# Hybrid decoder block on one core: query, key and all gate projections moved into seven-product units, attention heads moved behind them

## The chip, the cores and the metric

The kernel runs on one core of one Trainium2 chip. The metric is the device time in microseconds (us) of one execution, taken as the median of the runs. A core has five engines with a queue each, and each queue runs in order: TensorE (PE, matrix products and transposes; PEld is its load of the stationary operand), VectorE (DVE), ScalarE (ACT), GpSimd (POOL) and SyncE (SP), which issues every DMA of this kernel. Work on different engines meets only through semaphores.

## The reference, cut to what matters

One block, 1024 tokens, width 1024, float32:

```python
xn = rmsnorm(x, norm1_g)
qa, ka, va, qr, kr, vr, gr, gate_a, gate_b = [xn @ wl[:, bounds[i]:bounds[i + 1]] for i in range(9)]
qa = rmsnorm(qa.reshape(B, S, 12, 128), q_norm_g); ka = rmsnorm(ka.reshape(B, S, 12, 128), k_norm_g)
# three groups of four heads: query t attends keys t - j*dilation, (window, dilation) = (128,1), (512,4), (2048,16)
s = q @ k.T * 128**-0.5 - slope * distance        # -inf outside the window
m = max(s); p = exp(s - m); den = sum(p); o = p @ v / den; lse = m + log(den)
o_a = sum over the groups of softmax(lse over the groups) * o
o_r = groupnorm(retention(qr, kr, vr)) * silu(gr)
y = sigmoid(gate_a) * (o_a @ w_proj_a) + sigmoid(gate_b) * (o_r @ w_proj_b)
x = x + y @ w_out
x = x + square(relu(rmsnorm(x, norm2_g) @ w_up)) @ w_down
```

The combined projection `wl` has 12,800 columns: queries, keys and values of attention 1536 each, retention queries and keys 1024 each, retention values and its gate `gr` 2048 each, `gate_a` and `gate_b` 1024 each.

## The kernel before

**Products.** Each operand of a large product is held as two parts, a rounded one and the rest (`split`, L325 to L330: ACT writes the rounded part `wh` or `xh`, DVE subtracts for `wl` or `xl`), and each 128-deep term is three matmuls (`Pipe.group`, L229): high by high, high by low, low by high. All large matmuls carry line 229. `mm`, `ms` and `tr` are PSUM pools of three, two and three banks (`mm` 3, `tr` 2, `ms` 3).

**Two forms of a projection.** The plain form takes every term. The other is a unit of seven products for 256 output columns over all 1024 tokens: the token and depth halves of the input form sums and differences once (`differences`, operands `ES`), the weight quarters form theirs per unit (`sums`, L123), and the seven products N1 to N7 (`strassen_order`, `product`) are added up into the four quarters of the result. A product is 4 terms, 12 matmuls of 512 columns; a unit is 84 of them, where the plain form of the same columns takes 96. `Weights` loads, sums and splits the weights in the order that is written out for it, through three or four raw slots and six split buffers.

**Order.** PE runs in the order in which the program is written (`manual_schedule`); the other engines are ordered by a scheduler. `Pipe.at(lag, fn)` puts a small piece of work between the terms of a later step, so that PE has large matmuls to run while DVE and ACT prepare it. The stages up to the retention are these:

1. Attention: 12 heads (`heads`: slot by slot, groups 1, 2, 0), 8 blocks of 128 tokens each. A step computes queries, keys and values of one head and one block in plain form (24 matmuls, 384 columns). ACT sums the squares of queries and keys (L659), DVE and POOL make the root (L342, L343), DVE scales (L663), PE turns them (L669), ACT and DVE apply the gains (L671, L673). Two or nine steps later come the scores (L593), one step after that the turned exponentials (L606), then the values product (L613). Rows of results go to `acc_d` in DRAM; `load_heads` and `combine` (`weigh`, `mix`, `turn_mixed`) mix the three groups of a slot.
2. Three of the eight pairs of gates in plain form (`w_gate`, 12 steps of 24 matmuls), the sigmoid by ACT at once (`gate_out`, L698). The input's sums and differences are made here.
3. 21 units: 5 pairs of gates, 8 of retention queries and keys, 8 of the retention gate.
4. Retention, the two output projections (`w_pa`, and `pb` in units), `w_out`, the second norm, `up` in units, `down` in seven products.

Of the kernel before, what the change touches and what calls it, by code (L numbers as in the profile page):

```python
# [37 lines left out]
class Weights:  # L38
# [57 lines left out]
    def add_units(self, tag, srcs):  # L96
# [31 lines left out]
        for j in range(-1, len(srcs)):  # L128
            if j + 1 < len(srcs):
                r = base + 2 * (j + 1)  # L130
                piece((tag, j + 1, "A"), self.A[(j + 1) % 2], r + 1, both)
            if j >= 0:
                r = base + 2 * j
                piece((tag, j, "D"), (self.D, j % 2), r, slice(0, 512), lambda r=r: sums(r))
                piece((tag, j, "B"), self.B[j % 2], r + 1, both, lambda r=r: self.used.add(r + 1))
                piece((tag, j, "C"), self.C, r, both, lambda r=r: self.used.add(r))
        m = len(srcs)
# [139 lines left out]
def hybrid_block(ctx: ExitStack, tc: tile.TileContext, a: dict, out: bass.AP):  # L277
# [9 lines left out]
    big = pool(ctx, "big", 4)  # L287
# [15 lines left out]
    v_d = dram.tile([HEADS, S, DH], F, name="v_d")  # L303
# [9 lines left out]
    XS = {(j, i): slot_of(big) for i in range(2) for j in range(2)}  # L313
# [24 lines left out]
    const.tile([P, 224], F, name="rest")  # L338
# [88 lines left out]
    def dilated(g, b, src, dst):  # L427

        if g == 0:
            return src, dst[:, b * P:(b + 1) * P]  # L430
        r = 4 if g == 1 else 8
        src = src.rearrange("p (i r) -> p r i", r=r)
        if g == 1:
            nb, j = divmod(b, 4)
            return src, dst.rearrange("p (r i) -> p r i", r=r)[:, :, nb * P + 32 * j:nb * P + 32 * j + 32]
        return src, dst.rearrange("p (r i) -> p r i", r=r)[:, :, 16 * b:16 * b + 16]
# [4 lines left out]
    def load_heads(s, i, p2b):  # L441
        at = p2b.tile([P, 4, 3, DH + 2], F, name="at", bufs=1)
        rows = acc_d[512 * i:512 * i + 512].rearrange("(t p) (g s) e -> s p t g e", p=P, s=SLOTS)
        for t in range(4):
# [3 lines left out]
    def combine(s, i, p2b, at):  # L448
# [3 lines left out]
        return [lambda: weigh(p2b, at, st), *(lambda t=t: mix(t, at, st) for t in range(4)),  # L452
                lambda: turn_mixed(s, i, p2b, st)]

    def weigh(p2b, at, st):
        w = st["w"] = p2b.tile([P, 6, 4], F, name="w")
        st["o"] = p2b.tile([P, 4, DH], F, name="oa")
# [23 lines left out]
    def turn_mixed(s, i, p2b, st):  # L481
        pt = tr.tile([P, 4, P], F, name="tr")
        for t in range(4):
            nc.tensor.transpose(pt[:, t, :], st["o"][:, t, :], ident)
        ot = p2b.tile([P, 512], F, name="oaT")
        nc.scalar.activation(ot, pt.rearrange("p t q -> p (t q)"), AF.Copy)
        nc.sync.dma_start(oa_d[s, :, 512 * i:512 * i + 512], ot)
# [11 lines left out]
    attn = ExitStack()  # L499
    p3 = pool(attn, "p3", 2, "right")  # L500
    p2 = pool(attn, "p2", 2, "right")
    cpa = pool(attn, "cpa", 1, "right")
    with ExitStack() as ph:
        cp = pool(ph, "cp", 1)
        first = ExitStack()
        px = pool(first, "px", 2)
        cmb = None

        g1 = cp.tile([P, D], F, name="g1")
        gq = cpa.tile([P, HEADS], F, name="gq")  # L510
        gk = cpa.tile([P, HEADS], F, name="gk")
        dist = cp.tile([P, 2, 2 * P], F, name="dist")
        row = px.tile([P, D], F, name="xn", bufs=3)
        ones = cp.tile([1, P], F, name="ones")
        xts = {}

        def load_x(t):
            xts[t] = px.tile([P, D], F, name="xt", bufs=3)
            nc.sync.dma_start(xts[t], a["x"][t * P:(t + 1) * P, :])

        xts[0] = px.tile([P, D], F, name="xt", bufs=3)
        for cs in halves():
            nc.sync.dma_start(xts[0][:, cs], a["x"][0:P, cs])
        nc.sync.dma_start(row[0:1, :], a["norm1_g"][None, :])
        nc.sync.dma_start(ident, a["c_ident"])
        W.load()
        W.load()
        load_x(1)
        W.load()
        ss = px.tile([P, 4], F, name="ss")  # L530
        xn = px.tile([P, D], F, name="xn", bufs=3)
        lo, hi = halves()
        gp = [mm.tile([P, 512], F, name="mm") for _ in range(2)]
        with tc.manual_schedule(engines={mybir.EngineType.DVE, mybir.EngineType.Activation}):
            nc.vector.memset(ones, 1.0)
            nc.scalar.activation(ss[:, 3:4], half[:, 0:1], AF.Square)
            for cs, pm in zip(halves(), gp):
                nc.tensor.matmul(pm, ones, row[0:1, cs], start=True, stop=True)
            nc.scalar.activation(xn[:, lo], xts[0][:, lo], AF.Square, accum_out=ss[:, 0:1])
            nc.vector.tensor_tensor_reduce(xn[:, hi], xts[0][:, hi], xts[0][:, hi], op0=OP.mult, op1=OP.add,  # L540
                                           scale=1.0, scalar=0.0, accum_out=ss[:, 1:2])
            nc.vector.tensor_tensor(ss[:, 0:1], ss[:, 0:1], ss[:, 1:2], op=OP.add)
            rsqrt(ss[:, 2:3], ss[:, 0:1], 1.0 / D)
            nc.vector.tensor_copy(g1[:, lo], gp[0])
            nc.vector.scalar_tensor_tensor(xn[:, lo], xts[0][:, lo], ss[:, 2:3], g1[:, lo], op0=OP.mult, op1=OP.mult)
            W.pump(1)
            nc.scalar.activation(g1[:, hi], gp[1], AF.Copy)
            nc.vector.scalar_tensor_tensor(xn[:, hi], xts[0][:, hi], ss[:, 2:3], g1[:, hi], op0=OP.mult, op1=OP.mult)
            put_transposed(xn, 0, 0)
            W.pump(1)  # L550
            put_transposed(xn, 0, 1)
            W.pump(1)
        load_x(2)
        load_x(3)
        W.pump(1)

        def norm1(t):
            if t not in xts:
                load_x(t)
            ss = px.tile([P, 4], F, name="ss")  # L560
            xn = px.tile([P, D], F, name="xn", bufs=3)
            nc.scalar.activation(xn, xts[t], AF.Square, accum_out=ss[:, 0:1])
            rsqrt(ss[:, 1:2], ss[:, 0:1], 1.0 / D)
            nc.vector.scalar_tensor_tensor(xn, xts[t], ss[:, 1:2], g1, op0=OP.mult, op1=OP.mult)
            pipe.at(t - 1 - pipe.slot, *[lambda q=q: put_transposed(xn, t, q) for q in range(2)])

        norm1(1)
        pipe.at(0, lambda: W.pump())
        nc.sync.dma_start(gq, a["q_norm_g"])
        nc.sync.dma_start(gk, a["k_norm_g"])  # L570
# [896 lines left out]
```

## Time and profile before

| | |
|---|---|
| median of 3 runs | 2252.63 us (2251.44 to 2254.21) |
| the profiled execution | 2252.3 us, its span 2250.5 us, mean granted clock 0.998 |
| attention, from the first large matmul to the first gate | 10.95 to 521.16 us |
| three plain pairs of gates | 521.16 to 594.62 us |
| 21 units (and the first step of the retention's values among them) | 594.62 to 999.93 us |
| the rest | 999.93 to 2250.5 us |

The span is the time from the first to the last instruction that the profile holds; the device time lies 1.8 us above it. A row of a group gives busy time and the mean of one instruction. Large matmuls overlap in the pipeline, so their means (about 390 ns) are longer than the distance from one start to the next, and it is this distance that sets the time. A wait is put down to what ended it.

### The profile page before, as it was taken

To read this page: it belongs to the slowest core of one execution; us is meant where nothing else is said; L and a number is where in the kernel's file an instruction comes from. 1 tells how busy PE (TensorE), PEld (TensorE's weight loads), DVE (VectorE), ACT (ScalarE), POOL (GpSimd) and SP (SyncE) were. 2 spreads that over 40 slices of the span, in tenths; PEclk is the share of its full clock that TensorE was granted. 3 is DMA by queue.
4 is the path that set the end of the run, shared out by engine and by line. 5 is a ranking of instruction groups with operands and counts; after the bars stand their busy time and mean duration, and the time that the engine had idled before them with its cause. 6 is when DMAs were issued, how large, how long until landed. Compare 5 with 4: busy or idle time off the path is not lost. (4 is left out here: it accounts for less than half of the span.)

```text
span 2250.5 us, 30672 instructions
## 1 busy us (share of the span) xinstructions
PE 2212.8 (98%) x10772; PEld 1892.7 (84%) x10772; DVE 1352.6 (60%) x2570; ACT 1047.7 (47%) x2352; POOL 398.7 (18%) x436
## 2 busy tenths in 40 slices
PE   8999999999999999999999999999899999999999
PEld 7999999998888888888888877777788888778787
DVE  6444545454644445557777767783755556777874
ACT  5444434445343333345555544442555555754542
POOL 1111111110000000001222130000000000677873
PEclk9999999999999999999999999999999999999999
DMA  4313222322233333253563477774345556744432
GB/s 150 99 49 102 72 82 87 104 86 94 71 113 113 113 113 113 103 175 101 152 194 111 127 238 272 263 234 163 107 125 152 154 155 196 236 149 172 173 127 103
DMA packets 247852, 311.64 MB, mean 138 GB/s; under 512 B 15377, under 2 KB 171409, under 8 KB 247698
## 3 DMA queue, kind: packets, MB, share of 16 engines
q1 hardware_dynamic: 247698, 309.69, 42.7%
q8 instruction: 84, 1.38, 0.2%
q14 instruction: 70, 0.57, 0.1%
HBM read 209.92 MB, written 99.71 MB: 138 GB/s over the span
## 5 line engine op out<-in xcount | busy, mean ns | idle before, releaser
L330 DVE TENSOR_TENSOR wl<-raw,wh 128x1024 fp32r<-128x1024 f32 (+2 forms) x290 | 316.8, 1095 | 362.0 <-ACT wh L327 360.4
L229 PE MATMUL mm<-wh,xh 128*128 128x384 f32 (+1 forms) x1226 | 482.2, 393 | 1.7 <-ACT xh L327 1.2
L229 PE MATMUL mm<-wh,xl 128*128 128x384 f32 (+1 forms) x1226 | 439.3, 358 | 2.0 <-DVE xl L330 2.0
L327 ACT ACTIVATE wh<-raw 128x1024 fp32r<-128x1024 f32 (+2 forms) x290 | 273.1, 944 | 359.6 <-PE ms L229 107.5
L229 PE MATMUL mm<-wl,xh 128*128 128x384 f32 (+1 forms) x1226 | 437.8, 357 | 0.0
L229 PE MATMUL mm<-xh,wh 128*128 128x512 f32 x720 | 281.9, 391 | 4.1 <-ACT ms L397 4.1
L229 PE MATMUL mm<-xl,wh 128*128 128x512 f32 x720 | 281.0, 390 | 0.3 <-DVE xl L330 0.3
L229 PE MATMUL mm<-xh,wl 128*128 128x512 f32 x720 | 280.7, 390 | 0.0
L229 PE MATMUL ms<-xh,wh 128*128 128x512 f32 x700 | 275.9, 394 | 3.1 <-DVE St L896 1.6
L229 PE MATMUL ms<-xh,wl 128*128 128x512 f32 x700 | 272.6, 389 | 0.0
L229 PE MATMUL ms<-xl,wh 128*128 128x512 f32 x700 | 272.6, 389 | 0.0
L229 PEld LDWEIGHTS mm<-wh,xl 128*128 128x128 f32 x1226 | 230.8, 188 | 22.7 <-DVE xl L330 3.4
L229 PEld LDWEIGHTS mm<-wh,xh 128*128 128x128 f32 x1226 | 232.0, 189 | 21.1 <-ACT xh L327 1.7
L229 PEld LDWEIGHTS mm<-wl,xh 128*128 128x128 f32 x1226 | 232.8, 190 | 16.8
L229 PEld LDWEIGHTS mm<-xh,wh 128*128 128x128 f32 x720 | 135.6, 188 | 34.2 <-ACT ms L397 6.2
L229 PEld LDWEIGHTS mm<-xl,wh 128*128 128x128 f32 x720 | 135.6, 188 | 28.6 <-DVE xl L330 0.7
L229 PEld LDWEIGHTS mm<-xh,wl 128*128 128x128 f32 x720 | 135.6, 188 | 28.4
L229 PEld LDWEIGHTS ms<-xh,wh 128*128 128x128 f32 x700 | 131.5, 188 | 32.6 <-ACT u L405 2.5
L229 PEld LDWEIGHTS ms<-xh,wl 128*128 128x128 f32 x700 | 131.4, 188 | 27.6
L229 PEld LDWEIGHTS ms<-xl,wh 128*128 128x128 f32 x700 | 131.5, 188 | 26.2
L343 POOL TENSOR_TENSOR ssa<-ssa,half 128x2 f32<-128x2 f32 x96 | 66.7, 694 | 427.1 <-DVE ssa L342 410.1
L882 POOL TENSOR_TENSOR st<-st,half 128x1 f32<-128x1 f32 x32 | 27.5, 858 | 645.5 <-DVE st L881 645.4
(300 smaller groups left out, 3663.7 us busy)
## 6 DMA issues: line engine op xcount, KB each, us to landing
raw<-in_w_att SPq DMA_DIRECT2D x48, 384.0 KB, 4.0
raw<-in_w_up SPq DMA_DIRECT2D x32, 512.0 KB, 3.9
h_d<-s SPq DMA_DIRECT2D x64, 256.0 KB, 4.4
raw<-in_w_down SPq DMA_DIRECT2D x32, 512.0 KB, 4.3
s<-sg_d SPq DMA_DIRECT2D x40, 256.0 KB, 4.0
xh<-h_d SPq DMA_DIRECT2D x11, 896.0 KB, 4.5
s<-on_d SPq DMA_DIRECT2D x36, 256.0 KB, 5.2
xl<-h_d SPq DMA_DIRECT2D x10, 896.0 KB, 4.5
```

What stands on the lines that cost most here:

```text
L229: self.nc.tensor.matmul(ps, x, y, start=start, stop=stop, skip_group_check=not first)
L327: hi = nc.scalar.activation(dst_h, src, AF.Copy)
L330: nc.vector.tensor_tensor(dst_l, src, dst_h.bitcast(F), op=OP.subtract)
L343: nc.gpsimd.tensor_tensor(dst, dst, half[:, :w], op=OP.pow)
L882: nc.gpsimd.tensor_tensor(st[:, 9:10], st[:, 8:9], half[:, 0:1], op=OP.pow)
```

## The change

- **Values first.** The values of all 12 heads are now computed at the start in plain form, 512 columns (four heads) at a time: 3 x 8 steps of 24 matmuls (`w_av`, `values`), and written to `v_d` in DRAM.
- **Units.** Queries and keys of a head are one unit (`w_aqk_q`, 12 units). Then come 8 units of the retention gate, 8 of all gate pairs (`NG` is now 8), 8 of retention queries and keys: 36 units in all. The split buffers `B` are taken in the other order (`flip`).
- **Norm of queries and keys.** A unit gives them already turned (features by tokens). ACT copies the quarter in the order of the group's dilation into `sg`, which goes to `qk_d` in DRAM; ACT squares it, `split` parts the square, and two matmuls with a 0/1 matrix `pick` add the 128 features up into one of 48 rows of a PSUM bank. After the last of them one root of the 48 x 512 block is taken by ScalarE, with a correction step on DVE, and goes to `rs_d`.
- **Heads between.** From product 138 of the 252 on, head after head every 9 products: `bring` loads a half of queries or keys and its roots (the same row for all partitions), `scale` multiplies both and the gain in one DVE instruction, `fetch` loads one block of values; a block's scores are put between the terms of one product, its turned exponentials three products later, its values product two after that, in one bank with the turn of a later block. Biases come ready from DRAM. The minimum of negated scores replaces the maximum. `combine` works on two blocks instead of four. Rows of results are stored block by block.
- **Gates.** The gates go to DRAM without the sigmoid; ACT applies it where they are used, in the stages of `w_pa` and `pb`.
- **One quarter of the input** (`XS[0, 1]`, high and low part) is given up during the units: it is written to `xs_d` and loaded again after them.

```diff
-    for slot, g in heads:
+    for n in range(3):
         for u in range(4):
-            W.add(a["w_att"][g * SLOTS + slot, u])
-    for d, bufs in enumerate([(0, 1), (2, 4), (3, 5)]):
-        for u, b in enumerate(bufs):
-            W.add(a["w_gate"][d, u], b)
-    NG, NQ = KT - 3, 2 * RH
-    W.add_units("in", [a["w_gate_q"][j] for j in range(NG)] + [a["w_rqk_q"][j] for j in range(NQ)]
-                + [a["w_gr_q"][j] for j in range(8)])
+            W.add(a["w_av"][n, u])
+    NA, NG, NQ = HEADS, KT, 2 * RH
+    W.add_units("in", [a["w_aqk_q"][j] for j in range(NA)] + [a["w_gr_q"][j] for j in range(8)]
+                + [a["w_gate_q"][j] for j in range(NG)] + [a["w_rqk_q"][j] for j in range(NQ)], 1)
...
+            pm = values(us, ts, t == NT - 1, ms, "ms")
+            vt = vp.tile([P, 512], F, name="vt")
+            nc.scalar.activation(vt, pm, AF.Copy)
+            nc.sync.dma_start(v_d[n, ts], vt)
...
+        def scores():
+            sp = tr.tile([P, 4, P], F, name="tr")[:, :nk].rearrange("p a b -> p (a b)")
...
+                nc.tensor.matmul(sp[:, to], q, qk[1][c][:, (n0 - 4 * c) * P:(n1 - 4 * c) * P], start=True, stop=True)
...
+            nc.vector.tensor_tensor_reduce(s[:, :w], sp, bias[:, 2 * P - w:], op0=OP.add, op1=OP.min,
+                                           scale=1.0, scalar=3.0e38, accum_out=acc[:, DH:DH + 1])
+            nc.scalar.activation(s[:, :w], s[:, :w], AF.Exp, scale=-1.0, bias=acc[:, DH:DH + 1],
+                                 accum_out=acc[:, DH + 1:DH + 2])
...
+    FIRST, EACH, PAIR = 138, 9, 2
...
+                x = core.tile([P, 512], F, name="qk"[f] + "T", bufs=2)
+                rb = core.tile([P, 512], F, name="rb", bufs=2)
+                for j in range(2) if r > 1 else (c,):
...
+                    for dst, src in ((x, qk_d[n, f, j][:, cs]), (rb, roots)):
+                        if r > 1:
+                            dst = dst.rearrange("p (r j i) -> p j r i", r=r // 2, j=2)[:, j]
+                            src = src.rearrange("p (r i) -> p r i", r=r // 2)
+                        nc.sync.dma_start(dst, src)
...
+            nc.vector.scalar_tensor_tensor(x, x, gqk[:, f, h:h + 1], rb, op0=OP.mult, op1=OP.mult)
...
+                on(p0 - 4 + 4 * c, lambda n=n, c=c: bring(n, c))
+                for f in range(2):
+                    on(p0 - 2 + 4 * c + f, lambda n=n, c=c, f=f: scale(n, c, f))
+            for b in range(NT):
+                p, m = p0 + b, NT * n + b
+                on(p, lambda n=n, b=b: fetch(n, b))
+                on(p, lambda n=n, b=b: begin(n, b))
+                on(p, lambda m=m: pipe.at(3, lambda: turned(m)))
+                on(p, lambda m=m: pipe.at(0, stages[m][0]))
...
+                for c, y in enumerate(hl):
+                    nc.tensor.matmul(to, pick[:, P - 1 - m:2 * P - 1 - m], y, start=sums["n"] + c == 0,
+                                     stop=sums["n"] + c == 8 * HEADS - 1)
...
+                    nc.scalar.activation(w[:k], y[:k], AF.Sqrt)
...
+    XS[0, 1] = slot_of(pool(ctx, "x01b", 1))
+    for i, x in enumerate(XS[0, 1]):
+        nc.sync.dma_start(x.bitcast(F).rearrange("p a b -> p (a b)"), xs_d[i])
...
+            nc.scalar.activation(gates[n], gates[n], AF.Sigmoid)
             nc.vector.tensor_tensor(gates[n], gates[n], pp, op=OP.mult)
...
             sgb, y, *pa = ahead.pop(n)
+            nc.scalar.activation(sgb, sgb, AF.Sigmoid)
```

PE in the middle of the heads, before: scores (`qT`, `kT`), exponentials (`pr`) and values (`Vd`, `V`) stand one by one between terms of 384 columns.

```order
L613 MATMUL ms<-Vd,pT 128x128
L229 MATMUL mm<-wh_2113,xh 128x384
L229 MATMUL mm<-wl_2114,xh 128x384
L229 MATMUL mm<-wh_2113,xl 128x384
L606 MATMUL ms<-ident,pr 128x128
L229 MATMUL mm<-wh_2113,xh 128x384
L229 MATMUL mm<-wl_2114,xh 128x384
L229 MATMUL mm<-wh_2113,xl 128x384
L593 MATMUL ms<-kT,qT 128x128
```

PE in the middle of the heads, after: `V` and `s` (values product of one block, turn of another) and scores (L642), now in the two `tr` banks.

```order
L229 MATMUL ms<-xh,wl_1187 128x512
L660 MATMUL tr<-V,pT 128x128 x2
L653 MATMUL tr<-ident,s 128x128
L229 MATMUL ms<-xh,wh_1186 128x512
L229 MATMUL ms<-xl,wh_1186 128x512
L229 MATMUL ms<-xh,wl_1187 128x512
L642 MATMUL tr<-kT,qT 128x128
L229 MATMUL ms<-xh,wh_1186 128x512
L229 MATMUL ms<-xl,wh_1186 128x512
L229 MATMUL ms<-xh,wl_1187 128x512
L488 MATMUL tr<-ident,oa 128x128 x2
```

The large terms are 512 columns wide and belong to units; the turns of queries and keys (L669) are gone, and scores, turns and values moved from the `ms` banks to the `tr` banks.

ACT where the first heads begin, before: sigmoids of the plain gates (L698) between the last exponentials (L600), with loads of function tables.

```order
L698 ACT_TABLE_LOAD
L698 ACTIVATE sg<-ms 128x512
L600 ACT_TABLE_LOAD
L600 ACTIVATE pr,acc<-s,acc 128x256
L671 ACTIVATE qT<-tr,gq 128x128
L615 ACTIVATE acc<-ms 128x128
L600 ACTIVATE pr,acc<-s,acc 128x128
```

ACT there, after: the last sigmoids of the retention gate (L815) between the first exponentials (L647); L821 copies raw gates, L655 and L661 copy out of the `tr` banks.

```order
L815 ACT_TABLE_LOAD
L815 ACTIVATE sg<-u_4275 128x512
L655 ACTIVATE pT<-tr 128x128
L647 ACT_TABLE_LOAD
L647 ACTIVATE s,acc<-s,acc 128x256
L821 ACTIVATE sg<-mm 128x512
L655 ACTIVATE pT<-tr 128x256
L647 ACTIVATE s,acc<-s,acc 128x128
L330 ACTIVATE wh_1186<-raw_4095 128x512
L815 ACT_TABLE_LOAD
L815 ACTIVATE sg<-ms 128x512
L661 ACTIVATE acc<-tr 128x128
```

The meeting of sigmoids and exponentials moved from the end of the heads to their beginning, and there are 12 table loads in the program where there were 7.

SP in the middle of the heads, before: whole heads are stored and loaded (`v_d`, `Vd`), with weights and `at` for the mix.

```order
L682 DMA v_d<-V 128x8x128
L182 DMA raw_5123<-in_w_gate 128x1024
L685 DMA Vd<-v_d 128x4x128 x2
L445 DMA at<-acc_d 128x3x130 x4
L487 DMA oa_d<-oaT 128x512
L182 DMA raw_5542<-in_w_gate 128x1024
```

SP in the middle of the heads, after, at a head of the third group (stride 8): halves of queries, keys and roots (L697) in runs of 64 elements, one block of `V` and of `acc` at a time, results of units (L823) and weights (L182) among them.

```order
L697 DMA rb<-rs_d 128x4x64 x2
L823 DMA rqk_d<-u_7076 128x512
L182 DMA raw_7486<-in_w_rqk_q 128x1024
L711 DMA V<-v_d 128x128
L662 DMA acc_d<-acc 128x130
L697 DMA qT<-qk_d 128x4x64 x2
L697 DMA kT<-qk_d 128x4x64
L711 DMA V<-v_d 128x128
```

The queue now carries the heads' many short transfers beside those of the units, 1328 DMAs in the whole program where there were 930.

More of the change, by code (lines that the diff above doesn't have):

```diff
@@ L496, in mix_next @@
                 pipe.at(1, mixing.pop())
[L499 to L529, printed above, removed]
+    x01, gst, tst = ExitStack(), ExitStack(), ExitStack()
@@ L530, in hybrid_block, with norm1 @@
+    load_x(2)
+    load_x(3)
+    W.pump(1)
+    def norm1(t):
+        if t not in xts:
+            load_x(t)
         ss = px.tile([P, 4], F, name="ss")
         xn = px.tile([P, D], F, name="xn", bufs=3)
[L532 to L565, printed above, removed]
@@ L691, in hybrid_block @@
+    assert not pipe.due
+    tst.close()
+    x01.close()
     nc.sync.dma_start(maskT, a["c_mask"])
@@ L1400, in _constants @@
     far = np.where((d >= 0) & (d <= P) & (k >= P) & (d % 2 == 0), d, BIG)
-    dist = np.stack([near, far], 1).astype(np.float32)
+    bias = []
+    for h in range(HEADS):
+        g = h // SLOTS
+        bias.append((near if g < 2 else far) * (2.0 ** (-8.0 * (h + 1) / HEADS) * (DIL[g] if g < 2 else 8)))
     mask = np.zeros((P, RH, P), np.float64)
@@ L1411, in _constants @@
         "c_ident": np.eye(P, dtype=np.float32),
-        "c_dist": dist,
+        "c_bias": np.stack(bias).astype(np.float32),
         "c_mask": mask.astype(np.float32),
@@ L1427, in _layout @@
     gates = [np.concatenate([r(GA + d * P, P), r(GB + d * P, P)]) for d in range(KT)]
+    order = [g * SLOTS + slot for slot in range(SLOTS) for g in (1, 2, 0)]
     a = {
```

465 lines of the change are left out of this document (263 added, 202 removed).

## The prediction

> **What bounds the kernel now.** I read the page's first part, then the waits of TensorE, then the time line of PE at the borders of the stages, then the groups by shape, and last DVE, ACT and DMA by stretches.
>
> ```profile
> span 2250.5 us, 30672 instructions
> PE 2212.8 (98%) x10772; PEld 1892.7 (84%) x10772; DVE 1352.6 (60%) x2570; ACT 1047.7 (47%) x2352; POOL 398.7 (18%) x436
> ```
>
> PE is busy for all but 37.7 us of the span, so time leaves this kernel when PE gets less to do, and comes in where PE is made to wait. Its waits before are few:
>
> ```profile
> engine line waited for: us in total, times, longest us
> PE tr L1102 <- DVE x L1122: 5.9, 1, 5.9
> PE mm L538 <- DMA xn<-in_norm_g: 5.0, 1, 5.0
> ...
> PE mm L229 <- DVE xl L330: 2.3, 5, 1.1
> ```
>
> The change rewrites what lies between the first large matmul and the start of the retention. PE's time line gives the borders:
>
> ```profile
> 10.95 0.67 PE L229 MATMUL mm<-wh,xh 128*128 128x384 f32 x1
> ...
> 17.26 0.33 PE L229 MATMUL mm<-wh,xh 128*128 128x384 f32 x1
> ...
> 18.30 0.33 PE L229 MATMUL mm<-wh,xh 128*128 128x384 f32 x1
> ...
> 594.62 0.39 PE L229 MATMUL mm<-xh,wh 128*128 128x512 f32 x1
> ...
> 999.93 0.39 PE L229 MATMUL mm<-wh,xh 128*128 128x512 f32 x1
> ```
>
> From 17.26 to 18.30 there are six matmuls of 384 columns with nothing between: 0.1733 us each, from start to start. From 594.62 to 999.93 there are 21 units of 84 and 24 of the retention's values, 1788 matmuls of 512 columns: 405.31 / 1788 = 0.2267 us. Per column both forms cost nearly the same, so what counts is the number of columns and the small pieces between:
>
> ```profile
> L669 PE MATMUL tr<-ident,qk 128*128 128x128 f32 x192 | 36.5, 271 | 0.0
> L606 PE MATMUL ms<-ident,pr 128*128 128x128 f32 x140 | 30.9, 272 | 0.4 <-ACT sg L698 0.4
> L613 PE MATMUL ms<-Vd,pT 128*128 128x128 f32 x160 | 28.1, 274 | 0.0
> L593 PE MATMUL ms<-kT,qT 128*128 128x256 f32 x88 | 26.4, 382 | 0.9 <-DVE pT L608 0.9
> L593 PE MATMUL ms<-kT,qT 128*128 128x128 f32 x104 | 19.9, 273 | 0.0
> L613 PE MATMUL ms<-V,pT 128*128 128x128 f32 x120 | 18.7, 275 | 0.2 <-ACT sg L698 0.2
> ```
>
> The program issues 80 products with `Vd` and the trace holds 160: a plain product of two float32 operands runs as two passes, a turn as one. Counted in passes of 128 columns the heads have 192 + 140 + 160 + 2 x 88 + 104 + 120 = 892, with 24 turns of mixed rows 916, and 56 turns of the input fall in this stretch: 972. Between 10.95 and 594.62 lie 583.7 us; 2304 matmuls of 384 take 399.3, the 288 of the plain gates 65.3, and I take off some 5 us of waits and of the slow first matmuls. That leaves 114 us: 0.1175 us for a pass.
>
> **The parts, on PE.**
>
> Main products. Before: 2304 x 0.1733 + 288 x 0.2267 + 405.3 = 869.9 us. After: 576 for the values, 36 units x 84 = 3024, and the same 24: 3624 x 0.2267 = 821.6. Gain 48.3 us. Fewer products are the reason (15 units more, each 84 matmuls where the plain form has 96: 180 x 0.2267 = 40.8); the rest is the wider form.
>
> Small pieces. The 192 turns of queries and keys go; scores, turns, values and mixes stay (280 + 140 + 280 + 24 = 724 passes, also where a score is cut at column 512). 192 x 0.1175 = 22.6 us gained.
>
> Sums of squares. 48 x 2 matmuls with `pick`, 512 columns: 96 x 0.2267 = 21.8 us lost. Together PE is rid of 49.1 us.
>
> **What hides the rest.** Units and heads now share the time. Three heads are 27 products, 324 x 0.2267 = 73.4 us, and a quarter of the small passes, 181 x 0.1175 = 21.3: 94.7 us. The nearest durations:
>
> ```profile
> L1167 DVE SCALAR_TENSOR_TENSOR xn<-y,ssq,g 128x512 f32<-128x512 f32 x8 | 6.0, 752 | 4.9 <-POOL ssq L343 4.9
> L596 DVE CUSTOM_DVE_ANT_0 s<-ms,bias 128x256 f32<-128x256 f32 x44 | 18.6, 423 | 14.8 <-PE ms L593 14.4
> L478 DVE SCALAR_TENSOR_TENSOR oa<-at,w,oa 128x128 f32<-128x128 f32 x64 | 23.1, 361 | 1.8
> L468 DVE TENSOR_TENSOR w<-w 128x4 f32<-128x4 f32 x16 | 2.6, 163 | 0.6
> L600 ACT ACTIVATE pr<-s,acc 128x256 f32<-128x256 f32 x44 | 22.2, 505 | 48.0 <-DVE acc L598 40.8 <-PE tr L669 7.1
> L600 ACT ACTIVATION_READ_ACCUMULATOR pr<-s,acc 128x1 f32 x96 | 18.0, 187 | 0.0
> ```
>
> and the stretches (columns: length, then busy us and instructions of PE, PEld, DVE, ACT and POOL, clock, DMA share, GB/s), one of units, three of retention, one of the `up` stage with its start:
>
> ```profile
> 620.00:660.00 40.00, 40.00 (x178) 33.13 (x177) 16.49 (x20) 15.74 (x24) 0.00 (x0) 1.00 0.33 122
> 1000.00:1100.00 100.00, 98.79 (x483) 81.74 (x482) 73.01 (x173) 52.97 (x111) 20.20 (x25) 1.00 0.55 158
> 1100.00:1200.00 100.00, 99.77 (x487) 82.70 (x486) 74.04 (x176) 53.60 (x114) 21.50 (x26) 1.00 0.48 145
> 1200.00:1300.00 100.00, 99.37 (x483) 82.32 (x483) 75.54 (x155) 56.78 (x117) 24.28 (x29) 1.00 0.42 125
> 1600.00:1800.00 200.00, 193.63 (x859) 159.36 (x858) 124.58 (x173) 105.89 (x168) 2.03 (x3) 0.98 0.45 136
> ```
>
> DVE in 94.7 us: the units 41% of 73.4 = 30; 24 scores at no more than 0.5 with their read-out, 11; 12 `scale` at 0.75, 9; four mixes of two blocks, each 16 tiny steps at 0.163, two scalings and four 0.361 steps, some 18. That is 68 us, 72%. ACT: units 39% of 73.4 = 29; 24 exponentials at up to 0.69 with read-out, 15; 48 copies out of `tr`, which read as much as an exponential without its sum, at about 0.3, 14; mixes 3: 61 us, 64%. Neither is the bound. In the unit stretch PE never waits, in the retention, with DVE as full as this, it loses 2.07 us of 300. The 12 heads last 4 x 94.7 = 379 us: from 0 to, by the last of these rows (6.37 of 200, or 3.2%), some 12. I take 5, above the retention's 2.6, because a score's bank must be read by DVE within one product.
>
> Other edits. The heavier first step (raw weights of 512 KB, splits of 1024 columns instead of 768) delays the start by 0 to 3 us, but DVE loses the work on queries and keys in that stage, and the waits for `xl` (2.3 us, quoted above) lie mostly there; I take +1. The reload of `XS[0, 1]`, twice 1 MB on SP's queue ahead of the first retention loads, needs about 6 us of all DMA engines while one step of values (5.4 us) covers them: 0 to 5, I take +2. The 40 late sigmoids, 0.6 us of ACT each, stand ahead of DVE work in stages where ACT is under 55%: 0 to 4, I take +1.5. They replace sigmoids that ACT did at once, so ACT's total stays. POOL's 96 roots go from a place that never held PE. The table loads:
>
> ```profile
> 528.26 1.28 ACT L698 ACT_TABLE_LOAD   x1
> 529.55 0.60 ACT L698 ACTIVATE sg<-ms 128x512 f32<-128x512 f32 x1
> ```
>
> Five more at 1.28 us are 6.4 us of ACT, most of them in the 17 us where the first heads meet the last sigmoids. Turns come three products (8 us) after their scores, so this stays inside the 5 us. The Trainium skill, ScalarE: Activation LUTs, section "Table sets: the hidden batching unit", counts about 2.7 us for a load; by that figure the five would be some 13 us, an estimate, and the trace's 1.28 decides.
>
> Sum against the profiled execution (2252.3, span 2250.5): -49.1 + 5 + 1 + 2 + 1.5 = -39.6, so 2212.7. The median shown is 0.3 us higher: 2213.
>
> **Rivals.**
>
> *Short transfers become the bound (ends slower).* A head of the third group brings queries, keys and roots in runs of 64 elements, 256 bytes: 16 DMAs of 512 packets, 8192, or 512 for each of 16 engines. No row of before has payload packets this short. The nearest, first large packets, then packets of 512 and 520 bytes (count, MB, share of the engines):
>
> ```profile
> DMA packets 8810, 21.17 MB, mean 106 GB/s; under 512 B 979, under 2 KB 979, under 8 KB 8799
> q1 hardware_dynamic: 8799, 21.02, 30.3%
> ...
> DMA packets 3487, 1.71 MB, mean 171 GB/s; under 512 B 166, under 2 KB 3487, under 8 KB 3487
> q1 hardware_dynamic: 3487, 1.71, 65.1%
> ```
>
> The first is 600 to 800 us: 0.303 x 200 x 16 / 8810 = 110 ns for 2.4 KB. The second is 1010 to 1020 us: 0.651 x 160 / 3487 = 29.9 ns for 490 bytes. The straight line through both gives 20 ns at 256 bytes; I take 20 to 30 ns, 10 to 15 us a head. The rest of such a head (units 33% of 24.5 us, 2048 packets of values and results, mixes) needs about 14 us, and the head lasts 31.6, so 24 to 29 us fit. They stop fitting above 34 ns a packet, and above 54 ns the four heads give back all that PE gained. The Trainium skill, DMA: Bandwidth & Descriptors, section "Specifications", says that below 512 bytes a transfer is done as read-modify-write; no run here shows what that costs. As a mechanism of this kernel, a read added to each write doubles the 29.9 ns: 512 x 59.8 = 30.6 us a head, 13 over, 52 in four heads, 2265 us. Against it: these packets end in SBUF and come from DRAM runs of 1 KB, and the trace's prices fall with the bytes. Chance 0.15 for DMA or SP lateness that costs 35 us or more, most of it slower than before.
>
> *Each score a small stall.* Scores alternate with turns in two `tr` banks, while before they had the three of `ms`. If DVE stands behind a weight split that waits for ACT, or behind `scale` waiting for its loads, the next score waits. At 0.25 us for each of 96 blocks it is 24 us instead of 5: 2232. For it: DVE and ACT queues of 64 to 72% with instructions up to 1.2 us. Against it: the retention at 74% stalls less than 1%. Chance 0.19.
>
> *No new waits at all.* The heads hide wholly and the reload too: 2250.5 + 1.8 - 49.1 = 2203, a little lower if the early waits for `xl` go too. Chance of under 2203: 0.06.
>
> That the gain does not arrive on PE is hardly a rival: PE is the bound, and products are counted out.
>
> **How the numbers follow.** The forecast, 2203 to 2222, has 0.60; small stalls, 2222 to 2247, 0.19; no waits, 0.06; late transfers, above 2247, 0.15, of which 0.04 within 0.2% of 2252.6 (about what a measurement here can tell from no change) and 0.11 slower. Faster is 0.85. The range that leaves out no more than 2 in 10 goes from 2199 to 2245.
>
> **What would show it.** PE instructions lose the 384-column form; 36 units at 0.227 us per matmul, between heads too, show the main term; the large matmuls begin the retention near 950 to 960 us. L669 is gone and `pick` costs about 22 us. PE waits named `tr` with DVE or ACT, beyond 10 us in all, would show the stall rival; DVE waits at `scale` for `rb` or `qT` from DMA, DMA near 1.0 in every third head, the transfer rival. I am wrong if the stretch up to the retention is shorter by clearly less than 40 us, or if a stage behind it grows by more than 5.

## The result, and the profile after

The changed kernel takes 2289.94 us (median of 4 runs, 2286.44 to 2290.46) against 2253.42 us before (4 runs, 2251.44 to 2257.71): a ratio of 1.0156, with a 95% interval of 1.0138 to 1.0174. It is slower by 36.5 us where the forecast was a gain of 39.6. The profiled execution took 2290.4 us, its span is 2288.6.

The page's first part, after:

```profile
span 2288.6 us, 29131 instructions
PE 2196.0 (96%) x9928; PEld 1792.8 (78%) x9928; DVE 1389.2 (61%) x2374; ACT 1138.0 (50%) x2145; POOL 330.2 (14%) x340
```

PE is busy 16.8 us less than before (2212.8), but stands for 92.6 us instead of 37.7. TensorE's waits, after (engine, line, what ended the wait: us in total, times, longest):

```profile
PE tr L653 <- ACT acc L661: 43.4, 94, 2.2
PE mm L229 <- ACT ms L398: 9.5, 7, 2.2
PE tr L1166 <- DVE x L1186: 5.9, 1, 5.9
PE ms L911 <- DMA rkT<-rqk_d: 5.3, 1, 5.3
PE mm L229 <- ACT ms L1358: 5.0, 3, 3.0
```

The first row is new, and it is one wait for nearly every block of the heads: the turn of the exponentials (L653) waits for ACT's copy of a values product (L661). It has nothing to do with the data that it turns. In the code of `turned`, the values product of block m - 2 goes to `bank[:, 0]`, then ACT copies it out, then the turn of block m goes to `bank[:, 1:]` of the same bank.

PE's time line at the borders, after: the first large matmul, and the second step of the retention's values (the first step runs among the last units, before and after).

```profile
11.77 0.78 PE L229 MATMUL ms<-wh,xh 128*128 128x512 f32 x1
...
1023.13 0.39 PE L229 MATMUL mm<-wh,xh 128*128 128x512 f32 x1
```

So the rewritten stretch lasts 1011.4 us, where it was 989.0; the forecast for it was 944.9 (989.0 - 49.1 + 5). What lies behind it lasts 1265.5 us of the span instead of 1250.6, where + 3.5 had been expected. That second difference is the less certain one: in five later profiles whose program is the same behind the border (e1, e4, e6, e9, e10) this part takes 1259.9 to 1269.0 us. The 77.7 us between forecast and profile are 66.5 in the stretch and 11.4 behind it, less 0.2 at the start.

The stretches, after (length, then busy us and instructions of PE, PEld, DVE, ACT and POOL, clock, DMA share, GB/s): first units alone, then 400 us with the heads.

```profile
150.00:400.00 250.00, 250.00 (x1099) 206.01 (x1098) 129.56 (x171) 152.23 (x224) 0.00 (x0) 1.00 0.30 100
...
550.00:950.00 400.00, 361.40 (x1740) 292.40 (x1739) 204.65 (x539) 192.99 (x492) 0.00 (x0) 1.00 0.61 173
```

In the units of this row PE never waits, as forecast. In the heads 38.6 of 400 us are lost although DVE is busy for 51% and ACT for 48%: no engine is full, and DMA is at 0.61. PE's time line shows one block:

```profile
704.19 0.39 PE L229 MATMUL mm<-xh,wl 128*128 128x512 f32 x1
704.42 0.38 PE L660 MATMUL tr<-V,pT 128*128 128x128 f32 x2
705.17 0.33 PE L653 MATMUL tr<-ident,s 128*128 128x128 f32 x1 [0.37 <-ACT acc L661]
705.26 0.48 PE L229 MATMUL mm<-xh,wh 128*128 128x512 f32 x1
```

and ACT's between them:

```profile
704.84 0.28 ACT L661 ACTIVATE acc<-tr 128x128 f32<-128x128 f32 x1 [1.86 <-PE tr L660]
```

ACT was idle for 1.86 us and took the copy as soon as it could. Yet PE has to finish its product, ACT has to read it, and only then the turn begins: 0.84 us from the product's start to the next large matmul. Only 0.37 of that is named as a wait, because the product counts as busy until its modelled end. Over the whole stretch the 98 such places (the 94 with a wait and four without) take 102.3 us from the first small matmul to the next large one.

### The profile page after: what moved, and what is told of

The parts are those of the page before. It is cut to its first block, busy times and chain, and to the rows that moved or that the text cites. A ratio compares the mean times of both kernels' runs of the same rounds, so it can differ in the third digit from the quotient of the medians.

```text
span 2288.6 us, 29131 instructions
## 1 busy us (share of the span) xinstructions
PE 2196.0 (96%) x9928; PEld 1792.8 (78%) x9928; DVE 1389.2 (61%) x2374; ACT 1138.0 (50%) x2145; POOL 330.2 (14%) x340
## 3 DMA queue, kind: packets, MB, share of 16 engines
q8 instruction: 78, 1.28, 0.2%
## 5 line engine op out<-in xcount | busy, mean ns | idle before, releaser
L333 DVE TENSOR_TENSOR wl<-raw,wh 128x1024 fp32r<-128x1024 f32 (+1 forms) x308 | 344.1, 1118 | 382.6 <-ACT wh L330 381.4
L330 ACT ACTIVATE wh<-raw 128x1024 fp32r<-128x1024 f32 (+1 forms) x308 | 295.5, 961 | 263.8 <-PE ms L229 92.9
L229 PE MATMUL mm<-xh,wh 128*128 128x512 f32 x960 | 389.9, 406 | 9.9 <-ACT ms L398 9.5
L229 PE MATMUL mm<-xh,wl 128*128 128x512 f32 x960 | 376.4, 392 | 0.0
L229 PE MATMUL mm<-wh,xh 128*128 128x512 f32 x458 | 187.3, 409 | 2.5 <-ACT xh L330 2.0
L229 PE MATMUL mm<-wh,xl 128*128 128x512 f32 x458 | 180.3, 394 | 0.3 <-DVE xl L333 0.3
L229 PE MATMUL mm<-wl,xh 128*128 128x512 f32 x458 | 179.3, 392 | 0.0
L229 PEld LDWEIGHTS mm<-wh,xl 128*128 128x128 f32 x458 | 86.5, 189 | 20.2 <-DVE xl L333 0.8
L229 PEld LDWEIGHTS mm<-wh,xh 128*128 128x128 f32 x458 | 86.8, 189 | 19.2 <-ACT xh L330 2.4
L229 PEld LDWEIGHTS mm<-wl,xh 128*128 128x128 f32 x458 | 87.0, 190 | 15.8
## 6 DMA issues: line engine op xcount, KB each, us to landing
h_d<-s SPq DMA_DIRECT2D x64, 256.0 KB, 4.3
qk_d<-sg SPq DMA_DIRECT2D x48, 256.0 KB, 2.5
s<-sg_d SPq DMA_DIRECT2D x40, 256.0 KB, 4.4
s<-on_d SPq DMA_DIRECT2D x36, 256.0 KB, 5.0
```

The source lines that it names most:

```text
L229: self.nc.tensor.matmul(ps, x, y, start=start, stop=stop, skip_group_check=not first)
L330: hi = nc.scalar.activation(dst_h, src, AF.Copy)
L333: nc.vector.tensor_tensor(dst_l, src, dst_h.bitcast(F), op=OP.subtract)
```

## The experiments

Each experiment ran beside the kernel before, e1 to e4 on one chip (before: 2255.47 us), e5 to e8 on a second (2254.27) and e9 to e11 on a third (2255.58); ratios are against these. e2, e3, e4, e6, e7 and e9 have one run each, so differences of a few us between them and others prove little.

**Theory 1**: the turn waits for ACT's copy because both use one bank, and PE runs empty each time. **Theory 2**: the turn comes too soon behind its own exponential. **Theory 3**: the two banks of `tr` (`mm` and `ms` have three each) are too few for scores, turns and values products.

**e1_copies_behind.** `turn` and `values` now give their ACT copies back as functions, and `turned` calls them behind both products:

```diff
+            copies = []
             if m >= 2:
-                stages[m - 2][2](bank)
+                copies.append(stages[m - 2][2](bank))
             if m < len(stages):
-                stages[m][1](bank)
+                copies.append(stages[m][1](bank))
+            for copy in copies:
+                copy()
```

> Edit: in each shared bank both PE groups (values product, then turn) are issued first and both ACT copies out of the bank behind them. Theory 1 (the turn waits for ACT's copy of the values product because both lie in one bank tile, and PE drains for it): the distance from L660 to the turn falls from 0.94 us to the 0.24 us that a small piece took in the kernel before, 94 times 0.68 us, about 65 us; the time falls from 2290 to 2215 to 2240 us, most likely 2225, and PE waits for acc are gone. Theory 2 (the turns come too early behind their exponentials): no change, 2284 to 2296, with the same wait under the exponential's name. Theory 3 (two banks are too few, so that PE waits for the bank to come free): no change either, 2284 to 2296, with a wait at the values product or the scores.

Measured: 2230.72 us (2224.69 to 2232.75) against 2255.47 before, ratio 0.9885, interval 0.9865 to 0.9905. Putting ACT's copy behind the turn instead of ahead of it makes the change 1.1% faster where it was 1.6% slower. TensorE's waits of this kernel begin with

```profile
PE mm L229 <- ACT ms L398: 11.3, 6, 3.7
PE tr L1175 <- DVE x L1195: 5.9, 1, 5.9
PE ms L920 <- DMA rkT<-rqk_d: 5.5, 1, 5.5
```

and none is for `acc`. One block on PE's time line, the same three lines as above (L663 is now the values product):

```profile
701.55 0.39 PE L229 MATMUL mm<-xh,wl 128*128 128x512 f32 x1
701.78 0.38 PE L663 MATMUL tr<-V,pT 128*128 128x128 f32 x2
702.00 0.27 PE L653 MATMUL tr<-ident,s 128*128 128x128 f32 x1
702.03 0.47 PE L229 MATMUL mm<-xh,wh 128*128 128x512 f32 x1
```

0.25 us instead of 0.84. The 98 places take 38.3 us instead of 102.3: 64.0 us. The stretch itself shrinks by the same amount:

```profile
10.70 0.78 PE L229 MATMUL ms<-wh,xh 128*128 128x512 f32 x1
...
958.01 0.39 PE L229 MATMUL mm<-wh,xh 128*128 128x512 f32 x1
```

947.3 us against 1011.4. Theory 1 holds; theories 2 and 3 had forecast no change.

**e2_turn_later.** The changed kernel with one more product between scores and turn (a fourth `s` buffer; a spare tile of 200 columns is dropped for the space, here and in the next one):

```diff
-                on(p, lambda m=m: pipe.at(3, lambda: turned(m)))
+                on(p, lambda m=m: pipe.at(4, lambda: turned(m)))
...
```

> Edit: the changed kernel with the turn four products behind its scores in place of three; the order inside a bank is as in the changed kernel. Theory 1 (wait for the copy in the same bank): no change, 2284 to 2296 us, and the named wait of the turn for acc stays at 40 us or more. Theory 2 (turn too early behind its exponential): 2225 to 2255 us. Theory 3 (too few banks): no change.

Measured: 2311.34 us in its one run. The wait of the turn, in the view of TensorE's waits:

```profile
PE tr L652 <- ACT acc L660: 43.7, 94, 3.6
```

More distance changes nothing at the wait; theory 2 falls. That the kernel is 21 us slower than the changed one, 8.5 us of it in the stretch and 13.1 behind it, none of the theories forecast. 2.9 of these us are a longer wait for the retention's first loads; the rest one run leaves open.

**e3_turn_first.** The changed kernel with the two pieces of a bank in the other order (and a third `pT` buffer):

```diff
-            if m >= 2:
-                stages[m - 2][2](bank)
             if m < len(stages):
                 stages[m][1](bank)
+            if m >= 2:
+                stages[m - 2][2](bank)
```

> Edit: the changed kernel with the turn ahead of the values product in each bank, each still followed by its copy. Theory 1: a wait of the same size, now at the values product for ACT's copy of the turn (pT), which is longer (up to 256 columns): 2280 to 2310 us. Theory 2: the turn keeps its wait, for s, and the values product has none; 2284 to 2296 us. Theory 3: waits at scores or turn for the bank, none at the values product.

Measured: 2321.62 us, a little above the range. The wait has gone over to whichever piece comes second, and is longer, as the copy of the turn is:

```profile
PE tr L659 <- ACT pT L654: 53.3, 94, 4.1
```

The 98 places take 117.2 us for 102.3. That is 15 of the 32 us over the changed kernel; the others are not explained.

**e9_every_other.** In e1_copies_behind, every second bank gets the old order back:

```diff
                 copies.append(stages[m - 2][2](bank))
+                if m % 2:
+                    copies.pop()()
```

> Edit: as e1_copies_behind, but in every other bank the copy of the values product stands ahead of the turn again, as in the changed kernel. Theory 1 with a price per wait: half of the 94 waits come back, 47 times 0.63 to 0.68 us, 30 to 32 us above e1_copies_behind: 2256 to 2264 us, waits of the turn for acc near 22 us. If the loss is a backlog that builds up only when every turn waits, less than half of it comes back: under 2250.

Measured: 2262.24 us, 31.5 above e1_copies_behind and inside the range for a price per wait, but in part by luck.

```profile
PE tr L653 <- ACT acc L667: 32.1, 47, 4.0
```

The 98 places take 80.7 us, 42.4 more than in e1_copies_behind, or 0.90 us for each of the 47 instead of 0.68, and 9 us of that come back in the stages behind, which the edit does not touch. The trace shows what makes a wait longer. As a rule (the median) ACT starts its copy 0.04 us after the product's modelled end. In 12 of the 47 waits it comes over 0.15 us late, 15.5 us in all, because it is at other work, such as a sigmoid with its table load or a split of weights; in the changed kernel that holds for 14 of the 94, 9.6 us in all. Without these delays the price is the same in both kernels: (42.4 - 15.5) / 47 = 0.57 us and (64.0 - 9.6) / 94 = 0.58 us a wait.

**e10_own_banks.** The changed kernel, with copies where they were, but the values product in a `tr` bank of its own:

```diff
-            bank = tr.tile([P, 4, P], F, name="tr")
             if m >= 2:
-                stages[m - 2][2](bank)
+                stages[m - 2][2](tr.tile([P, 4, P], F, name="tr"))
             if m < len(stages):
+                bank = tr.tile([P, 4, P], F, name="tr")
                 stages[m][1](bank)
```

> Edit: the changed kernel with the values product in a tr bank of its own, its copy still ahead of the turn, the turn in the next bank. Theory 1: the turn no longer depends on that copy; what is left is that scores, values product and turn now share two banks, each free only when its reader is done: 2225 to 2250 us. Theory 3 (too few banks): PE waits at the scores and the values product for acc, pT or s, 2260 to 2300 us.

Measured: 2241.29 us (2239.62 to 2247.01), ratio 0.9945 (0.9925 to 0.9965). The 98 places take 38.5 us, as in e1_copies_behind; in their place the scores now wait for their bank:

```profile
PE tr L642 <- ACT acc L661: 9.7, 9, 2.6
```

So it is the bank in common that makes the wait, and theory 3 is a real but small effect, which appears only with three uses of two banks per block. The Trainium skill, PSUM — Partial Sum Buffer, section "PSUM bank collisions raise a hardware error", gives the rule "Semaphore-guard PSUM by bank × quadrant (by bank is the simple version), not by address". By that rule the turn must wait here, although it writes other columns than ACT reads, and the rows agree: the wait is there for the second and third quarter of the bank while the first is read, and gone with another bank. A bank is one tile of the program here, so the runs do not tell whether the wait was set for the bank or for the tile. Whether the chip would bear it without the wait was not tried.

**e4_all_short_runs.** e1_copies_behind, with the short runs of the third group used for all heads:

```diff
-            r = strides(g)
+            r = 8
```

> Edit: as e1_copies_behind, and queries, keys and roots of all 12 heads are loaded in runs of 64 elements (256 bytes), not only those of the last four; the tokens of the other eight heads then stand in a wrong order, so the time alone counts. If a packet of 256 bytes costs 20 to 30 ns, all of it stays hidden: within 5 us of e1_copies_behind. If it costs 59.8 ns, each of the eight heads takes 13 us more than its 31.6 us: about 100 us above e1_copies_behind, with a DMA share near 1.0.

Measured: 2226.84 us, within the scatter of e1_copies_behind (the time alone counts here). Packets and queue share between 560 and 945 us, first of e1_copies_behind:

```profile
DMA packets 102466, 76.57 MB, mean 199 GB/s; under 512 B 38176, under 2 KB 86048, under 8 KB 102432
...
q1 hardware_dynamic: 102432, 76.16, 68.8%
```

then of this kernel:

```profile
DMA packets 143724, 76.74 MB, mean 199 GB/s; under 512 B 96000, under 2 KB 131328, under 8 KB 143690
...
q1 hardware_dynamic: 143690, 76.33, 72.0%
```

Nearly the same bytes in 41,258 more packets cost 3.2% of 385 us on 16 engines, 197 us, or 4.8 ns for each added packet (an estimate from these rows). This is not the price of a short packet, because each group of short ones replaces a longer one. The trace's records of single packets give that price: in this stretch of this kernel 88,064 packets of 256 bytes took 17.9 ns each on average, 11,520 of 512 bytes 30.5 ns. So the prediction's 20 to 30 ns was a little high, and its straight line (20 ns) close. The transfer rival is out: a doubled price, 59.8 ns, is not there.

**e5_sigmoid_at_once.** e1_copies_behind, with the gates' sigmoid where the unit ends:

```diff
-                nc.scalar.activation(sg, src, AF.Copy)
+                nc.scalar.activation(sg, src, AF.Sigmoid if n < NG else AF.Copy)
...
-            nc.scalar.activation(gates[n], gates[n], AF.Sigmoid)
...
-            nc.scalar.activation(sgb, sgb, AF.Sigmoid)
```

> Edit: as e1_copies_behind, with the gates' sigmoids undone: ACT applies the sigmoid when a unit gives its quarter, as before the change, and none in the stages of the two output projections. If the late sigmoids are what made the stretch from the retention's last turn to the second norm's first turn longer (252.7 us before, 257.8 in e1_copies_behind), it comes back to 252 to 254 and the time falls by about 5 us, to 2222 to 2227. Rival: the sigmoids now stand among the exponentials of the heads, up to 32 results with two table loads of 1.28 us each, 82 us more of ACT in a stretch where it is busy for half the time; then PE waits for ACT in the heads and the time rises to 2232 to 2260.

Measured: 2239.14 us (2238.48 to 2240.28), ratio 0.9935 (0.992 to 0.995). The time is in the rival's range, and the stretch that was named first did become shorter. The stretch from the retention's last turn to the second norm's first turn is 251.7 us, against 257.8 in e1_copies_behind and 252.7 before, the shortest of all. In ten profiles with late sigmoids and this part of the program unchanged it lies between 253.6 us (e9) and 259.9 (e2), so they cost 2 to 8 us there. But the loads of tables in the heads cost more; the groups of ACT by shape:

```profile
L647 ACT ACT_TABLE_LOAD x30 | 38.5, 1283 | 0.5
L831 ACT ACT_TABLE_LOAD x29 | 37.2, 1283 | 4.9 <-DMA sg_d<-sg 4.4
```

That is 75.7 us of ACT, against 5.1 for the 4 loads at L647 in the kernel it is compared with, and PE waits for copies behind them (scores for `pT` 8.5 us); retention's first scores come 18.6 us later. By the two ratios, moving the sigmoids behind the heads gains about 0.5%.

**e6_no_square_sums.** e1_copies_behind without the 96 `pick` matmuls and the root; queries and keys are not normed, rows of queries take the roots' place:

```diff
-            pipe.at(3, add)
+            if m % 4 == 3 and n % 3 == 2:
+                nc.sync.dma_start(rs_d[12 * (n // 3):12 * (n // 3) + 12], sg[:12])
```

> Edit: as e1_copies_behind, without the 96 matmuls with pick and without the root behind them; rows of queries stand in for the roots, so the norm of queries and keys is left out. By the prediction's term the 96 matmuls cost 96 times 0.2267, 21.8 us; with the waits of some 4 us around the root the time falls by 22 to 27 us against e1_copies_behind, to 2202 to 2208. If part of them ran in time in which PE waits anyway, it falls by less than 15.

Measured: 2204.24 us, span 2202.4 against 2227.0: 24.6 us. But only 19.3 of them are in the stretch (947.3 to 928.0 us); the others lie behind it in stages that the edit does not touch, and can't be counted for it. The 96 matmuls themselves take 22.2 us in e1_copies_behind, from the start of each pair to the next large matmul, so the term of 21.8 us stands. The stretch gains less because PE now waits elsewhere: 2.8 us between 150 and 400 us, where it never waited before.

**e7_retention_loads_apart** and **e8_both_mended.** e7: the first loads of retention queries and keys go through POOL's queue. e8: that, and DVE's five steps of the root in four pieces of 128 columns.

```diff
-                nc.sync.dma_start(qk[i], rqk_d[h, i,
+                (nc.gpsimd if n < 2 else nc.sync).dma_start(qk[i], rqk_d[h, i,
...
-                    nc.vector.reciprocal(root[:k], w[:k])
...
+                    for q in range(4):
+                        pipe.at(2 + q, lambda q=q: piece(slice(q * P, (q + 1) * P)))
```

> Edit: as e1_copies_behind, and the loads of retention queries and keys for the first two blocks are issued by POOL in place of SP. If SP's order makes them late (they stand behind the store of the last unit's result and a load of weights), the wait for rkT (5.5 us) and the slow matmuls behind it go, and the time falls by 4 to 9 us against e1_copies_behind. If the DMA engines are what is busy there (the reload of XS, twice 1 MB), the wait stays at 4 us or more and the time within 2 us.

> Edit: as e7_retention_loads_apart, and DVE's steps of the root (3.35 us for the reciprocal alone) are cut into four pieces of 128 columns, one per product. If each of these waits is real, PE's waits at the root fall from some 4 us to under 2 and the time is 6 to 12 us under e1_copies_behind: 2215 to 2224. If e7 brings nothing, 2224 to 2228.

Measured: e7 2223.13 us in one run; e8 2219.17 us (2218.66 to 2219.73), ratio 0.9845 (0.9829 to 0.9862), the fastest kernel of the study. In e7 POOL issues the first of these loads 2.3 us before the border (958.0 us), where SP issued it 2.7 us behind it (960.8). The wait of PE shrinks from 5.5 to 2.4 us (two waits), in e8 to 1.6, and the way from the border to the first scores from 7.7 to 4.3 and 2.8 us. So SP's order was a good half of the wait. What is left fits the second reason of the expectation: the DMA engines are nearly full there, with the reload of `XS[0, 1]`. Two stretches of e1_copies_behind, one in the wait and one behind it (the columns as above, DMA share last but one):

```profile
962.00:964.00 2.00, 0.00 (x0) 0.00 (x0) 0.00 (x0) 0.00 (x0) 0.00 (x0) 1.00 0.95 319
...
966.00:968.00 2.00, 2.00 (x9) 1.81 (x9) 0.93 (x4) 0.99 (x3) 0.00 (x0) 0.50 1.18 292
```

For the root in pieces the runs show next to nothing. PE's loss between 400 and 550 us falls from 4.1 us in e1_copies_behind to 2.2, but DVE is at the root from 427 to 435 us, and PE loses only 1.0 us there, 0.6 in e8. The other waits, 1.7 us at 466 and 1.4 at 505, are for copies of ACT that stand behind a split of weights which were still being loaded. The second one is gone in e8 without an edit at that place, and e6_no_square_sums, which has no root at all, still loses 2.2 us in this window.

**e11_gates_earlier.** e8_both_mended, loading gates and partial sums three results ahead in the `pb` stage:

```diff
-            fetch(n + 2)
+            fetch(n + 3)
```

> Edit: as e8_both_mended, and in the stage of the second output projection the gates and partial sums are loaded three results ahead instead of two. If ACT stands there at a sigmoid whose gate is not loaded yet (waits of ACT for s from sg_d, 2.3 us at 1335 us in e8_both_mended), the waits of PE for ACT's copies L398 (7.9 us in all) fall by 3 to 5 us and the time by as much, to 2214 to 2217. Rival: the ten buffers of that stage then run out and the loads come no earlier: 2217 to 2225.

Measured: 2219.98 us (2219.66 to 2222.35), ratio 0.9848 (0.9833 to 0.9863): no change, the rival. ACT still stands at the sigmoids for their gates (13 waits of 21.6 us in all became 16 of 28.2), and PE's waits for L398 are 9.1 us for 7.9. The buffers are the likely reason, but it was not shown; how the late sigmoids could be had without their cost is open.

## Why the prediction was wrong

- **Main products, small pieces, `pick`: right in their sum.** Without the wait of the turns the stretch lasts 947.3 us, where 944.9 were forecast, the retention begins at 958.0 ("near 950 to 960"), and units run at 0.2267 us a matmul with PE full. `pick` measured 22.2 us for 21.8. The start came 0.8 us later after, for + 1, but 0.2 us earlier in e1_copies_behind, with the same program up to there: a term of this size can't be told from scatter.
- **The step that failed: "What hides the rest", with its 5 us for the heads.** It asked whether DVE, ACT and DMA have the time, and they have. It did not ask what a small matmul has to wait for in its own bank. "Scores alternate with turns in two `tr` banks" was seen, and "a score's bank must be read by DVE within one product" priced; the values product and the turn in one bank, with ACT's copy between, were passed over, though the order of PE shows them in adjacent rows. In place of the 5 us there were 64.0 of the turns' waits, and some 7 of everything else (947.3 less 939.9 without any wait). Of these 7 about 1 is at the root, 3 are copies behind splits of late weights, and 1.2 lie between 550 and 940 us, where the heads run; the others can't be placed. "Turns come three products after their scores, so this stays inside the 5 us" was true of the exponential and beside the point.
- **The small-stall rival** had the nearest form (a stall per block), but another place (the score), another cause (DVE's backlog) and a third of the price (0.25 us for 0.68). By the prediction's own sign (waits named `tr` with ACT beyond 10 us: there are 43.4) this rival came true, yet its 2232 us were 58 too low. The copy alone takes 0.28 us; 96 of them, 27 us, was a lower bound that could be had blind. 0.68 us is the copy with PE's emptying before it and refilling behind, together 0.58, and a share of the few times when ACT comes late.
- **Reload and first retention loads: mis-sized.** Taken as + 2 of 0 to 5. From the border to the first scores it is 7.55 us after for 2.04 before, + 5.5, and then matmuls at half speed (below).
- **Late sigmoids: mis-sized.** + 1.5 of 0 to 4 was taken; that stretch grew by 3.3 us after (256.0 for 252.7) and by 5.2 in e1_copies_behind, and was 6.2 shorter again when they were taken out. The term rested on ACT's free time. How the sigmoids cost more is not shown: PE waits there for ACT's copies (L398), but before the longest of these waits (3.7 us in e1_copies_behind) ACT came from a split of weights for which DVE had been late, and only one, of 1.5 us, stands right behind a late sigmoid.
- **Table loads: right in price, nearly right in place.** They took 1.28 us each; the about 2.7 us of the Trainium skill, ScalarE: Activation LUTs, section "Table sets: the hidden batching unit", were not met in any run. In the changed kernel one load (from 573.95 us on) and its sigmoid came between a values product and ACT's copy of it, in the longest wait of the heads, 2.17 us; with the copies behind they were hidden. 59 of them in the heads, in e5_sigmoid_at_once, were not.
- **Short transfers: rightly set aside**, at a price (20 to 30 ns) a little above the measured 17.9.
- Behind the stretch some 6 us (retention + 4.0, from the second norm on + 2.1) have no cause shown but for the half speed of the first matmuls. They are no larger than the scatter of that part between profiles of the same program (1259.9 to 1269.0 us).

## What to carry to other kernels

Before small products of two steps are put into one PSUM bank, look in program order for a read by another engine between the writes: PE then runs empty once per block, here for 0.58 us, and longer when the reading engine is at other work; no share of busy time shows it. Issue all writes of the bank first and the reads behind them; here that alone was worth 59 us (2289.94 to 2230.72), more than the whole saving of products. When a run's time comes out as forecast, look whether it did so in the stretch that the edit touches: in e6 and e9 a part of the difference lay elsewhere.

## What the runs showed of the hardware

A wait of PE can be followed by slow matmuls. In e1_copies_behind PE stands for 5.46 us before the retention's first scores; then its granted clock is 0.50 and 512 columns take 0.43 us until 970.5, when the distance comes back to 0.23:

```profile
965.68 1.20 PE L920 MATMUL ms<-rqT,rkT 128*128 128x128 f32 x4 [5.46 <-DMA rkT<-rqk_d]
...
967.52 0.63 PE L229 MATMUL mm<-wl,xh 128*128 128x512 f32 x1
967.95 0.63 PE L229 MATMUL mm<-wh,xl 128*128 128x512 f32 x1
...
970.51 0.57 PE L229 MATMUL mm<-wh,xl 128*128 128x512 f32 x1
...
972.05 0.40 PE L229 MATMUL mm<-wh,xl 128*128 128x512 f32 x1
```

Nine large matmuls lose some 1.8 us by it, besides the wait. A shorter wait can do the same. In the changed kernel the longest wait of a turn, 2.17 us, was followed 0.6 us later by 3.4 us at a granted clock of 0.50; that is what lowers the mean clock of this row to 0.97:

```profile
550.00:600.00 50.00, 44.62 (x205) 36.17 (x204) 25.50 (x47) 30.78 (x58) 0.00 (x0) 0.97 0.49 140
...
576.06 0.33 PE L653 MATMUL tr<-ident,s 128*128 128x128 f32 x1 [2.17 <-ACT acc L661]
```

The other waits of the heads there, up to 1.74 us, left the clock at 1.00, and so did one of 2.11 us in e7_retention_loads_apart, at the retention's first scores. The trace's clock records suggest why: in the changed kernel the slow spells begin at 576.64, 1030.62, 1344.64 and 1399.26 us, whole multiples of 3.41 us apart, as if PE's work were judged in fixed stretches of 3.41 us. The 2.17 us lie within one such stretch, while a grid drawn in the same way through e7's records (from 1277.21 us back) cuts its 2.11 us in two. That is an inference from these times; no run tested it. The Trainium skill, TensorE: Matmul & The Clock Gate, section "What's actually happening", describes half the clock after an idle window of about 3.4 us and until PE has been busy for as long. The 5.46 us wait agrees with it, and so does e8_both_mended, whose two waits there are 1.0 us at most and which has no slow spell there. The 2.17 us wait does not: a stretch of that length in which PE still worked for over 1 us was enough.
